# Latent heads: q and k multiplied straight into transposed form, rotary columns eight heads at a time on VectorE, other banks

## The chip, the cores and the metric

The kernel runs on one core of a Trainium2 chip. The core has a matrix engine (TensorE, PE in the profile), two engines for elementwise work (VectorE, DVE; ScalarE, ACT), GpSimd (POOL), SyncE (SP), which issues most transfers, and 16 DMA engines. Matrix products read SBUF and write to eight PSUM banks; a matrix product takes a *stationary* operand of 128 x 128 and a *moving* one of 128 rows and up to 512 columns.

The metric is the time of one execution in microseconds (us) of device time; the time before is the median of three runs. Beside these there is one profiled execution, from which the trace comes.

## The reference

One encoder layer for 256 tokens of width 4096, all in float32. A combined projection of the normalised input gives a query latent (1024 columns), a key-value latent (512), a rotary key (64), q, k, v of a dilated attention (2048 each) and two gates. The part that the change touches is the latent attention of 16 heads:

```python
q_a = jnp.einsum('bsr,re->bse', rms_norm(c_q, g_q_latent[i]), w_uq[i])
q_a = q_a.reshape(B, S, MLA_HEADS, QK_NOPE + QK_ROPE)          # 16 heads, 128 + 64 columns
q_nope, q_pe = q_a[..., :QK_NOPE], apply_rope(q_a[..., QK_NOPE:], positions)
kv = jnp.einsum('bsr,re->bse', rms_norm(c_kv, g_kv_latent[i]), w_ukv[i])
kv = kv.reshape(B, S, MLA_HEADS, QK_NOPE + V_HEAD)             # 16 heads, 128 + 128 columns
k_nope, v_a = kv[..., :QK_NOPE], kv[..., QK_NOPE:]
k_pe = jnp.broadcast_to(apply_rope(k_rope, positions)[:, :, None, :], (B, S, MLA_HEADS, QK_ROPE))
y_a = mla_attention(jnp.concatenate([q_nope, q_pe], axis=-1),
                    jnp.concatenate([k_nope, k_pe], axis=-1), v_a)   # dense softmax
y_a = rms_norm(y_a.reshape(B, S, MLA_WIDTH), g_out_mla[i]) * jax.nn.silu(gate_a)
```

After it come the output projection, a gated embedding with a 4096 x 4096 gate, and a final norm.

## The kernel before

**Precision.** Every float32 operand is split in two parts, `hi` (rounded to the format that TensorE multiplies at its fast rate) and `lo` (the rest). `split` (line 244) does it with one ACT copy and one DVE subtraction. `mm` (262) makes three products of them: hi by hi, hi by lo, lo by hi. Weights arrive by DMA in `raw` buffers (four of them), are split, and are multiplied; a step of the weight stream is one `raw` buffer, as a rule 128 x 1024 values.

**Blocks.** The large projections run as blocks of 1024 columns (`Block`, 994). Most rows of a block are *plain* steps of eight products of 512 columns (in four banks); some pairs of rows are *fast* ones, which make seven products instead of eight out of sums of the operands (four banks more) and cost DVE more work. `spread` sets their order from the number of fast pairs (`FAST_QKV`, `FAST_G`, `FAST_O`), the number of leading plain steps (`LEAD_...`) and of closing ones. When the last fast step has run, `..._mid` adds the extra banks into SBUF; at the end `..._done` does the rest. The order of the stages is: dilated q, k, v (six blocks, `d_mid`, `d_done`); the latent columns (four narrower chunks, `done_a`), beside which the dilated heads run; four gate blocks; the latent heads; two half chunks and three blocks of the output projection, two half chunks more; the last gate.

**Who sets the order.** The program is written engine by engine in a fixed order that the kernel itself plans. `Clock` (67) keeps an estimate of each engine's time, and every operation is recorded through `emit`, so that all rows of the profile have line 176. Steps of the weight stream go one after the other; between their products `tick` resumes the small tasks (evictions, attention heads, norms) whose inputs should be ready by the estimate. A task that `yield`s waits for its turn; `flags`, `locks`, `take` and `give` hold what must come first and which bank is in use. `turned` hands out one of two banks for transposes.

**Latent columns.** `done_a(i)` (504) evicts a chunk of latent columns with the norm factor of x, transposes it on PE and multiplies by the gains into `cT["q"]` and `cT["kv"]`, which are both transposed: latent index on the partitions, tokens on the columns. The last call rotates the key on POOL (`rotate`, 340), computes the norm factors `rq` and `rkv`, transposes the rotated key twice over and sets the flag "latents".

**Latent heads.** For each of eight pairs of heads there is a chunk of `w_uq` (384 columns: two heads of 128 + 64) and one of `w_ukv` (512 columns). The latents are the stationary operand, the weights move; the results stand with tokens on the partitions. `done_uq(i)` (677) scales by `rqs`, rotates the 64 rotary columns of two heads on POOL, doubles them with an ACT copy, transposes them (four transposes) and splits them; `done_uk(i)` (710) scales and splits v and scales k. Then `attend` (571) runs one head: two transposes of q and two of k, a split of 512 columns, scores (three products for q and k, two for the rotary part, for each of two row tiles), softmax, transposes of the weights, output. The query chunk's evictions wait for heads two pairs back, since the buffers of a pair are used in turn.

**Other places touched.** `load_res` (917) loads the residual by POOL's queue for the output projection; `half_o`, `done_o` (959, 969) end its half chunks; `y_sums` (1136) makes the sums for the fast pairs of the output projection.

Of the kernel before, what the change touches and what calls it, by code (L numbers as in the profile page):

```python
# [11 lines left out]
F32 = mybir.dt.float32  # L12
# [6 lines left out]
P = 128  # L19
S = 256  # L20
# [189 lines left out]
def encoder_layer(ctx: ExitStack, tc: tile.TileContext, x, p, positions, g_mix, w_in, g_q_latent, w_uq,  # L210
# [129 lines left out]
    def rotate(dst, src, tmp, h):  # L340

        half = ROPE // 2
        for t in range(NT):
            c = cc[:, t].unsqueeze(1).to_broadcast([P, h, ROPE])
            s1 = ss[:, t, :half].unsqueeze(1).to_broadcast([P, h, half])
            s2 = ss[:, t, half:].unsqueeze(1).to_broadcast([P, h, half])
            nc.gpsimd.tensor_tensor(dst[:, t], src[:, t], c, op=ALU.mult)
            nc.gpsimd.tensor_tensor(tmp[:, t, :, :half], src[:, t, :, half:], s1, op=ALU.mult)
            nc.gpsimd.tensor_tensor(tmp[:, t, :, half:], src[:, t, :, :half], s2, op=ALU.mult)
        nc.gpsimd.tensor_tensor(dst, dst, tmp, op=ALU.add)  # L350

# [152 lines left out]
    def done_a(i):  # L504
        def task(ps):
# [20 lines left out]
            if i == 2:  # L526
                kv = slot("B0", [2, 4, S], F32R)
                cT["kv"] = kv[:, 0], kv[:, 1]
            for lo, key, o, m in {0: ((0, "q", 0, 2), (2, "q", 2, 1)), 1: ((0, "q", 3, 2), (2, "q", 5, 1)),
                                  2: ((0, "q", 6, 2), (2, "kv", 0, 1)), 3: ((0, "kv", 1, 2), (2, "kv", 3, 1))}[i]:  # L530
                tag = yield from turned()
                tp = bank(tag, [2, S])
                for k in range(m):
                    for t in range(NT):
                        nc.tensor.transpose(tp[:, k, t * P:(t + 1) * P], c[:, t, (lo + k) * P:(lo + k + 1) * P], ident)
# [7 lines left out]
            kpe, rk = slot("B7a", [2, NT, 2, ROPE]), slot("B7b", [NT, 2, ROPE])  # L543
            for t in range(NT):
                for d in range(2):
                    nc.gpsimd.tensor_copy(kpe[:, 1, t, d], c[:, t, 384:448])
            rotate(rk, kpe[:, 1], kpe[:, 0], 2)
            tot = stat(2 * NT).rearrange("p (a t) -> p a t", a=2)
            nc.vector.tensor_tensor(tot[:, 0], sums[:, 0], sums[:, 1], op=ALU.add)
            nc.vector.tensor_tensor(tot[:, 0], tot[:, 0], sums[:, 2], op=ALU.add)  # L550
            nc.vector.tensor_tensor(tot[:, 1], sums[:, 3], sums[:, 4], op=ALU.add)
            yield from rsqrt_mean(rq, tot[:, 0], Q_LORA)
            nc.vector.tensor_scalar(rqs, rq, (NOPE + ROPE) ** -0.5, None, op0=ALU.mult)
            yield from rsqrt_mean(rkv, tot[:, 1], KV_LORA)
# [16 lines left out]
    def attend(h, q_src, k_src, pe, v, y, dil):  # L571
# [4 lines left out]
        tag = yield from turned()  # L576
        tp = bank(tag, [4, P])
        for t in range(NT):
            nc.tensor.transpose(tp[:, t], q_src(t), ident)
            nc.tensor.transpose(tp[:, NT + t], k_src(t), ident)  # L580
        flags.add(("took", dil, h))
        yield
        yield from take(f"T{h % 2}")
        qk = slot(f"T{h % 2}", [2, 4 * P], F32R)
        split(qk[:, 0], qk[:, 1], tp.rearrange("p a b -> p (a b)"))
        give(tag)
        if dil:
            flags.add(("read", h))
        yield
# [3 lines left out]
        for t in range(NT):  # L593
            a = tuple(qk[:, i, t * P:(t + 1) * P] for i in range(2))
            b = tuple(qk[:, i, S:] for i in range(2))
            mm(s[:, t], a, b, True, pe is None)
            if pe is not None:
                both = pe[0]()[:, t * P:(t + 1) * P]
# [3 lines left out]
        give(f"T{h % 2}")  # L602
# [72 lines left out]
    pairs = {}  # L675

    def done_uq(i):
        def task(ps):
            if i == 0:
                E["q"] = slot("Ah2", [2, NT, 2, NOPE + ROPE])  # L680
                E["kq"] = slot("Al2", [2, 1024])
                E["pe"] = slot("T5", [2, 2, S], F32R)
            while i > 1 and not all(("scored", 0, 2 * i - 3 - n) in flags for n in range(2)):
                yield
            q, kq = E["q"][:, i % 2], E["kq"][:, i % 2]
            pairs[i] = {"q": q, "kq": kq}
            for t in range(NT):
                nc.scalar.activation(q[:, t].rearrange("p h c -> p (h c)"), ps[t], AF.Copy, scale=rqs[:, t:t + 1])
            give(*ps.tags)
            both = kq[:, 512:].rearrange("p (t h d r) -> p t h d r", t=NT, h=2, d=2)  # L690
            rotate(both[:, :, :, 0], q[:, :, :, NOPE:], both[:, :, :, 1], 2)
            yield
            nc.scalar.activation(both[:, :, :, 1], both[:, :, :, 0], AF.Copy)
            yield
            tag = yield from turned()
            tp = bank(tag, [2, S])
            for h in range(2):
                for t in range(NT):
                    nc.tensor.transpose(tp[:, h, t * P:(t + 1) * P], both[:, t, h].rearrange("p d r -> p (d r)"),
                                        ident)  # L700
            yield
            pe = E["pe"][:, i % 2]
# [1121 lines left out]
```

## Time and profile before

| | us |
|---|---|
| median of three runs | 1932.27 |
| the runs | 1930.42 to 1932.83 |
| the profiled execution | 1933.49 |
| its span, first to last instruction | 1931.7 |
| mean granted clock of TensorE in it | 0.997 |

The profiled execution's time holds its span and 1.8 us around it. In the profile's rows a name stands for all tiles with it, without numbers: `m`, `s`, `o`, `t` are banks, `Ah`, `Al`, `B`, `T` are places in SBUF with several uses, `hi` and `lo` parts of weights, `raw` weights as they came, `st` small statistics. A row of a timeline has the start, the duration, the engine, the operation with output and inputs, and in brackets the idle time of the engine before it with what ended that. Matmuls are pipelined: a row's duration is longer than the distance to the next start, so the distance is what counts. A row of the waits has the engine, the tile it worked on, what it waited for, the total, how often, and the longest. A row of the stretches has, for each engine, busy us and the number of instructions, then the granted clock, the DMA engines' share and GB/s.

### The profile page before, as it was taken

The numbers are of one execution on the slowest core, as the hardware profiler recorded it, in microseconds if no ns is written. First come the engines' busy times: TensorE is split into PE (matmuls) and PEld (weight loads), VectorE is DVE, ScalarE is ACT, GpSimd is POOL, SyncE is SP. The second block draws the span as 40 slices with busy tenths as digits, with TensorE's granted clock in tenths as the row PEclk, the third lists the DMA queues.
The fourth block names the chain that finished last, engine by engine and source line by source line (L and its number), as shares of the span: only waits on it lengthen the run. The fifth ranks groups of instructions, "written<-read, shape, count | busy, mean of one in ns | idle before, by whom it ended". The sixth has DMA issues, their size and how long they took to land.

```text
span 1931.7 us, 25573 instructions
## 1 busy us (share of the span) xinstructions
PE 1902.9 (99%) x9227; PEld 1614.5 (84%) x9227; DVE 1639.1 (85%) x2270; ACT 1130.2 (59%) x1556; POOL 75.2 (4%) x123
## 2 busy tenths in 40 slices
PE   9999999999999999999999999999999999999997
PEld 7878888888899988888888888888888788888887
DVE  6999989998877789899998767898887989989865
ACT  7655556565577756556556656655555556666543
POOL 1000000000000110000001222100000000000000
PEclk9999999999999999999999999999999999999999
DMA  8666666666554566666666434766656566566665
GB/s 274 185 197 216 212 200 205 194 215 192 184 151 138 147 186 194 196 209 192 218 197 187 124 106 131 251 197 200 199 194 200 172 200 221 191 218 206 206 195 176
DMA packets 134191, 370.58 MB, mean 192 GB/s; under 512 B 11909, under 2 KB 45809, under 8 KB 133809
## 3 DMA queue, kind: packets, MB, share of 16 engines
q1 hardware_dynamic: 132176, 361.82, 59.6%
q0 software_dynamic: 1888, 7.14, 1.1%
q8 instruction: 72, 1.18, 0.3%
q14 instruction: 55, 0.44, 0.1%
HBM read 364.72 MB, written 4.19 MB: 191 GB/s over the span
## 4 chain that ended last, share of the span: by engine, by line
PE 80%; DVE 11%; issue 3%; ACT 3%; DMA 2%; POOL 1%; SPq 0%; DVEq 0%; ACTq 0%; POOLq 0%
PE m L176 44%; PE t L176 17%; PE s L176 10%; PE o L176 9%; DVE B L176 4%; DVE lo L176 3%; DVE T L176 1%; DVE Al L176 1%; ACT hi L176 1%; POOL Al L176 1%; DMA raw<-in_w_ple_gate_dram 1%; DMA raw<-in_w_in_dram 1%; DVE Ah L176 1%; ACT T L176 1%; DVE st L176 1%
## 5 line engine op out<-in xcount | busy, mean ns | idle before, releaser
L176 ACT ACTIVATE hi<-raw 128x1024 fp32r<-128x1024 f32 (+3 forms) x486 | 467.4, 969 | 347.0 <-PE m L176 107.8
L176 DVE TENSOR_TENSOR lo<-raw,hi 128x1024 fp32r<-128x1024 f32 (+3 forms) x486 | 537.9, 1115 | 137.2 <-ACT hi L176 133.8
L176 PE MATMUL m<-hi,Ah 128*128 128x512 f32 (+3 forms) x815 | 298.2, 380 | 0.9 <-ACT hi L176 0.9
L176 PE MATMUL m<-hi,Al 128*128 128x512 f32 (+3 forms) x807 | 289.7, 371 | 0.0
L176 PE MATMUL m<-lo,Ah 128*128 128x512 f32 (+2 forms) x702 | 261.8, 373 | 0.3 <-DVE lo L176 0.2
L176 PE MATMUL m<-hi,B 128*128 128x512 f32 (+2 forms) x772 | 244.7, 371 | 0.8 <-ACT Ah L176 0.4
L176 DVE TENSOR_TENSOR B<-raw,B 128x1024 fp32r<-128x1024 f32 (+2 forms) x209 | 189.0, 913 | 15.1 <-ACT B L176 13.2
L176 PEld LDWEIGHTS m<-hi,Ah 128*128 128x128 f32 x815 | 153.3, 188 | 22.9 <-ACT hi L176 1.6
L176 PEld LDWEIGHTS m<-hi,Al 128*128 128x128 f32 x807 | 151.4, 188 | 21.3 <-ACT hi L176 0.3
L176 ACT ACTIVATE B<-raw 128x1024 fp32r<-128x1024 f32 (+1 forms) x125 | 115.8, 934 | 80.5 <-DMA raw<-in_w_in_dram 22.4
L176 PEld LDWEIGHTS m<-hi,B 128*128 128x128 f32 x772 | 143.3, 188 | 21.1 <-ACT Ah L176 0.8
L176 PEld LDWEIGHTS m<-lo,Ah 128*128 128x128 f32 x702 | 132.2, 188 | 20.2 <-DVE lo L176 3.1
L176 PE MATMUL m<-lo,B 128*128 128x512 f32 (+2 forms) x386 | 142.2, 368 | 1.2 <-DVE lo L176 1.2
L176 PE MATMUL m<-B,Ah 128*128 128x512 f32 (+1 forms) x327 | 94.4, 382 | 0.0
L176 ACT ACTIVATE hi<-B 128x1024 fp32r<-128x1024 f32 x65 | 68.2, 1058 | 38.5 <-PE m L176 15.7
L176 DVE TENSOR_TENSOR lo<-B,hi 128x1024 fp32r<-128x1024 f32 x65 | 78.2, 1220 | 10.3 <-ACT hi L176 9.4
L176 DVE TENSOR_TENSOR T<-t,T 128x512 fp32r<-128x512 f32 (+2 forms) x73 | 49.8, 685 | 41.3 <-ACT T L176 40.9
L176 PE MATMUL t<-hi,Ah 128*128 128x512 f32 (+1 forms) x226 | 84.4, 388 | 0.0
L176 PEld LDWEIGHTS m<-lo,B 128*128 128x128 f32 x386 | 72.8, 189 | 11.5 <-DVE lo L176 2.3
L176 DVE TENSOR_TENSOR T<-raw,T 128x512 f32<-128x512 f32 (+2 forms) x101 | 77.6, 777 | 3.9 <-ACT T L176 2.5
L176 PE MATMUL t<-hi,Al 128*128 128x512 f32 x194 | 74.3, 392 | 0.0
L176 PE MATMUL t<-lo,Ah 128*128 128x512 f32 (+1 forms) x185 | 72.1, 390 | 0.0
(456 smaller groups left out, 3879.1 us busy)
## 6 DMA issues: line engine op xcount, KB each, us to landing
raw<-in_w_in_dram SPq DMA_DIRECT2D x320, 512.0 KB, 4.3
raw<-in_w_out_dram SPq DMA_DIRECT2D x128, 512.0 KB, 4.5
raw<-in_w_ple_gate_dram SPq DMA_DIRECT2D x128, 512.0 KB, 4.6
raw<-in_w_in_dram SPq DMA_DIRECT2D x48, 384.0 KB, 3.3
raw<-in_w_uq_dram SPq DMA_DIRECT2D x32, 384.0 KB, 3.3
raw<-in_w_ukv_dram SPq DMA_DIRECT2D x16, 512.0 KB, 3.9
raw<-in_w_in_dram SPq DMA_DIRECT2D x16, 448.0 KB, 3.5
T<-in_x_dram POOLq DMA_DIRECT2D x8, 512.0 KB, 9.8
```

The lines of the kernel that those rows point to most:

```text
L176: return do(out, *rest, **named)
```

## The change

For each pair of heads `query_unit` and `key_unit` take the place of the two chunks. In them the weights of one head are the stationary operand and the transposed latents move (256 columns, one per token), so that q and k come out transposed and the transposes and the split in `attend` fall away for the latent heads; v comes out as before. The loads of `w_uq` take the 128 columns of each head by themselves (rows of 512 bytes, two DMAs a step). A step here is a pair of steps that share a product: the first only loads and splits, the second multiplies both. `turn_steps` multiplies the rotary columns of eight heads at once, in four steps after pairs 0 and 4 (rows of 256 bytes, two DMAs a step); its `done` rotates them on DVE from the banks, doubles and transposes them for four heads at a time; for the second eight heads it waits until the heads whose place it takes have been scored. `rotate` on POOL is gone; the key is rotated on DVE. Instead of scaling q, its norm factor goes into the softmax (a product on DVE for the maximum, a scale in the exponential); that of kv is applied to the latent before its transposes, which therefore come later in `done_a`.

Besides: the banks of the gates, the heads and the output projection are dealt out in another order; the first block of q has three closing plain steps for two; the first gate block has four fast pairs for five and 14 leading steps for 12; the residual of two chunks is loaded earlier; `done_o` releases its banks before the squares; `y_sums` starts after the second rotary run and uses other places.

```diff
@@ done_a
+                T7["held"] = slot("B7a", [4, HD])
+                for t in range(NT):
+                    nc.scalar.activation(T7["held"][:, t], c[:, t, 256:384], AF.Copy)
+            if i == 3:
+                nc.vector.tensor_tensor(own, c[:, :, 384:], cc, op=ALU.mult)
...
+                yield from rsqrt_mean(rkv, tot[:, 1], KV_LORA)
+                for t in range(NT):
+                    nc.scalar.activation(c[:, t, :384], c[:, t, :384], AF.Copy, scale=rkv[:, t:t + 1])
+                    nc.vector.tensor_scalar(held[:, t], held[:, t], rkv[:, t:t + 1], None, op0=ALU.mult)
...
-            rotate(rk, kpe[:, 1], kpe[:, 0], 2)
@@ attend
+            nc.vector.tensor_tensor(nmax, nmax, rqs, op=ALU.mult)
             for t in range(NT):
-                nc.scalar.activation(e[:, t], s[:, t], AF.Exp, bias=nmax[:, t:t + 1], accum_out=l[:, t:t + 1])
+                nc.scalar.activation(e[:, t], s[:, t], AF.Exp, bias=nmax[:, t:t + 1], scale=rqs[:, t:t + 1],
+                                     accum_out=l[:, t:t + 1])
@@ query_unit
+        def load(r, j):
+            for h in range(2):
+                nc.sync.dma_start(r.rearrange("p a (b c) -> p (a b) c", c=2 * NOPE)[:, :, h * NOPE:(h + 1) * NOPE],
+                                  src[4 * P * j:4 * P * (j + 1), 2 * i + h, :NOPE].rearrange("(k p) c -> p k c", p=P))
+
+        def product(held, ps):
+            for h in range(2):
+                for kt in range(8):
...
+                    mm(ps[0][:, h], w, [q[:, kt] for q in cT["q"]], kt == 0, kt == 7)
+                    tick()
@@ key_unit
+        def product(held, ps):
+            for h in range(2):
+                for kt in range(4):
...
+                    mm(ps[0][:, h], w, [q[:, kt] for q in cT["kv"]], kt == 0, kt == 3)
+                    tick()
             for t in range(NT):
...
+                    mm(ps[1][:, t].rearrange("p (h c) -> p h c", h=2), [q[:, kt, t * P:(t + 1) * P] for q in cT["kv"]], w,
+                       kt == 0, kt == 3)
@@ turn_steps
+                for k in range(2):
+                    kt = 2 * j + k
+                    nc.sync.dma_start(box[0][:, k].rearrange("p (h r) -> p h r", h=8),
+                                      src[kt * P:(kt + 1) * P, 8 * n:8 * (n + 1), NOPE:])
...
+                nc.vector.tensor_tensor(own, ps[t], turn[2], op=ALU.mult)
+                nc.vector.tensor_tensor(other[..., :half], ps[t][..., half:], turn[0], op=ALU.mult)
+                nc.vector.tensor_tensor(other[..., half:], ps[t][..., :half], turn[1], op=ALU.mult)
+                give(tags[t])
+                twice = slot("T1", [8, 2, ROPE])
+                nc.vector.tensor_tensor(twice, *(a.unsqueeze(2).to_broadcast([P, 8, 2, ROPE]) for a in (own, other)), op=ALU.add)
+                yield
+                for j in range(2):
+                    while n and not all(("scored", 0, 4 * j + m) in flags for m in range(4)):
+                        yield
@@ load_res
-        while not all(("head", 0, h) in flags for h in range(HEADS)):
+        before = {6: ("pe", 1), 7: ("scored", 0, HEADS - 1)}.get(c)
+        while not (before in flags if before else all(("head", 0, h) in flags for h in range(HEADS))):
@@ y_sums
-        while not {("yT", 3), ("uq", 7)} <= flags:
+        while not {("yT", 3), ("pe", 1)} <= flags:
@@ the order of the stages
-    FAST_G, LEAD_G = (5, 7, 7, 7), (12, 6, 6, 4)
+    FAST_G, LEAD_G = (4, 7, 7, 7), (14, 6, 6, 4)
...
-        order = spread(FAST_QKV[n], LEAD_QKV[n], (2, 2, 2, 2, 2, 5)[n])
+        order = spread(FAST_QKV[n], LEAD_QKV[n], (3, 2, 2, 2, 2, 5)[n])
...
     for i in range(8):
-        for ch in (Chunk(cols(w_uq, 384 * i, 384), 8, 384, lhs_c("q"), ("m0", "m1"), done_uq(i), lambda j: ["latents"]),
-                   Chunk(cols(w_ukv, 512 * i, 512), 4, 512, lhs_c("kv"), ("m2", "m3"), done_uk(i),
...
+        steps.extend(query_unit(i, *next_banks(1)))
+        if i in (0, 4):
+            steps.extend(turn_steps(i // 4, next_banks(2)))
+        steps.extend(key_unit(i, next_banks(2)))
```

More of the change, by code (lines that the diff above doesn't have):

```diff
@@ L534, in task @@
                     for t in range(NT):
[L535 removed]
+                        nc.tensor.transpose(tp[:, k, t * P:(t + 1) * P], block(t, lo + k), ident)
                 yield
@@ L692, in task @@
[L692 to L702, printed above, removed]
-            nc.scalar.activation(pe, tp, AF.Copy)
@@ L960, in task @@
         def task(ps):
-            while c not in x1:
-                yield
+            yield from awaited(("res", c))
             for t in range(NT):
```

262 lines of the change are left out of this document (166 added, 96 removed).

## The prediction

> **What bounds the kernel now.** I read the engine totals first, then the stretches, then what TensorE (PE) waited for, then single places in order of time.
>
> ```profile
> PE 1902.9 (99%) x9227; PEld 1614.5 (84%) x9227; DVE 1639.1 (85%) x2270; ACT 1130.2 (59%) x1556; POOL 75.2 (4%) x123
> ```
>
> PE is the bound almost everywhere; VectorE (DVE) is the only engine close behind. The stretches show where PE is not full, and where DVE is:
>
> ```profile
> core 0: us, PE busy (x) PEld busy (x) DVE busy (x) ACT busy (x) POOL busy (x), PEclk, DMA share, GB/s
> 100.00:200.00 100.00, 97.48 (x423) 80.25 (x422) 97.71 (x129) 55.89 (x65) 0.00 (x0) 0.98 0.65 209
> ...
> 300.00:400.00 100.00, 100.00 (x442) 82.82 (x442) 93.28 (x108) 58.38 (x61) 0.00 (x0) 1.00 0.66 206
> ...
> 900.00:1000.00 100.00, 100.00 (x442) 82.58 (x441) 93.63 (x110) 60.81 (x64) 0.00 (x0) 1.00 0.65 202
> ...
> 1100.00:1200.00 100.00, 96.98 (x579) 87.06 (x579) 66.83 (x108) 60.65 (x130) 25.79 (x44) 1.00 0.41 123
> ...
> 1033.80:1209.00 175.20, 169.25 (x1000) 152.27 (x998) 126.26 (x200) 109.59 (x229) 41.98 (x69) 1.00 0.44 133
> ```
>
> PE loses time after 100 and from 1033.8 to 1209, the latent heads: 5.95 us idle there, with GpSimd (POOL) at work. In that stage DVE has 48.9 us free, ACT 65.6. In the dilated blocks and the gates (100:200, 300:400, 900:1000) DVE has only 2 to 7 us free in 100. The waits of PE over the whole span, largest first:
>
> ```profile
> PE t L176 <- ACT Al L176: 3.7, 5, 1.0
> PE o L176 <- DVE B L176: 2.5, 1, 2.5
> PE m L176 <- DVE lo L176: 2.2, 3, 1.2
> PE t L176 <- DVE T L176: 1.9, 3, 1.3
> ...
> PE m L176 <- DVE Al L176: 0.7, 1, 0.7
> PE s L176 <- DVE T L176: 0.6, 2, 0.4
> ...
> PE s L176 <- ACT T L176: 0.3, 1, 0.3
> ```
>
> So a change can win little by waits: these are 12 us, beside 2 at the start. What it does to the PE's own work decides as much.
>
> **PE's own work.** The pitch (start to start) of each kind of matmul, from places where nothing waits:
>
> ```profile
> 1120.46 0.51 PE L176 MATMUL m<-hi,B 128*128 128x384 f32 x2
> ...
> 1121.50 0.33 PE L176 MATMUL m<-hi,B 128*128 128x384 f32 x1
> ...
> 1123.55 0.60 PE L176 MATMUL t<-ident,T 128*128 128x128 f32 x4
> 1123.90 0.42 PE L176 MATMUL m<-hi,B 128*128 128x384 f32 x1
> ...
> 1886.19 0.28 PE L176 MATMUL m<-hi,Al 128*128 128x256 f32 x1
> ...
> 1888.35 0.28 PE L176 MATMUL m<-hi,Al 128*128 128x256 f32 x1
> ```
>
> Six matmuls of 384 columns start between the first two rows: 1.04/6 = 0.173 us. Four transposes take 0.35 us. Eighteen matmuls of 256 columns lie between the last two: 2.16/18 = 0.120. The stretch 300:400 has 512 columns alone: 100/442 = 0.226.
>
> Counted in the order of instructions before and after: 192 matmuls of 512 columns (keys and values) go; 96 of 512 (rotary columns, two runs of 48) come; the first gate block has one fast pair fewer, which is one product more, 3 of 512: net 93 fewer, -21.0 us. 384 of 384 columns go: -66.4. 768 of 256 come: +92.2. The two transposes of q and two of k per head go: 16 groups of four, -5.6. The rotary transposes stay at eight groups. Sum **-0.8 us**: the same columns are multiplied, in narrower pieces which cost 0.01 to 0.02 us more for each cut, and the transposes about pay for that. So "straight into transposed form" wins nothing in PE work, and the rest hangs on waits.
>
> **The rotary wait.** Before, each pair of heads sends its rotary columns over POOL; one pair, all engines:
>
> ```profile
> 1149.01 0.46 POOL L176 TENSOR_TENSOR Al<-Ah,cc 128x128 f32<-128x128 f32 x1 [13.54 <-ACT Ah L176]
> ...
> 1152.45 0.39 PE L176 MATMUL m<-hi,B 128*128 128x512 f32 x1
> 1152.63 0.72 POOL L176 TENSOR_TENSOR Al<-Al 128x256 f32<-128x256 f32 x1
> ...
> 1153.38 0.42 ACT L176 ACTIVATE Al<-Al 128x256 f32<-128x256 f32 x1 [1.80 <-POOL Al L176]
> ...
> 1153.86 0.66 PE L176 MATMUL t<-ident,Al 128*128 128x128 f32 x4 [1.01 <-ACT Al L176]
> ```
>
> POOL takes 4.3 us (1149.01 to 1153.35) for seven small operations; then ACT copies, then PE transposes, 1.2 us after it could have (1152.45 to 1153.86, less 0.23). The view counts 3.7 us in five such waits; counted from the last start, as here, instead of the last modelled end, I put 4.5 us on them. The change removes POOL and this copy: **-4.5**. The removed split of q and k (waits on T by s) gives **-0.9** (0.6 + 0.3).
>
> What takes its place on DVE, by the groups of the stretch 1033 to 1210:
>
> ```profile
> L176 DVE TENSOR_TENSOR T<-t,T 128x512 fp32r<-128x512 f32 x30 | 20.6, 688 | 21.4 <-ACT T L176 21.2
> ...
> L176 DVE TENSOR_SCALAR Al<-m,st 128x256 f32<-128x256 f32 x16 | 7.1, 478 | 2.2 <-PE m L176 1.1 <-ACT B L176 0.9
> L176 DVE SCALAR_TENSOR_TENSOR B<-m,st,B 128x256 fp32r<-128x256 f32 x16 | 6.9, 474 | 0.0
> ```
>
> Four rotations come (two runs, two row tiles), each one 512-wide, two 256-wide and one 1024-wide operation (at most twice a 512-wide): 0.7 + 0.9 + 1.4 = 3.0 us, 12 in all; also 24 splits of 512 (three a pair, 16.5) and 16 products of two columns, under 0.5 each. The 16 splits of q and k (11) and the last two groups (14) go. Net under +12 us of DVE in a stage with 48.9 free; ACT loses the copies and gets no more splits than DVE. Cover: the other weight matmuls. If it is gone, one 3.0 us rotation stands before a head. There are such places: the second run may write its transposed rotary queries only when heads 0 to 7 are scored, and head 8 waits for all of it. I take **+1**, between 0 and two rotations with their transposes (6).
>
> **The loads.** 16 loads of 512 KB with rows of 256 bytes (8 steps of two) and 32 with rows of 512 take the place of rows of 1536. The trace has no row for such packets. From 300:400, packets of 4096 bytes move 206/(0.66 x 16) = 19.5 GB/s per engine. If the rate held, a rotary step of 512 KB would cost 1.7 us; PE spends 12 x 0.226 = 2.7 on it. From above: if a short packet took as long as one of 1536 bytes at that rate (0.079 us), 2048 of them on 16 engines would take 10.1 us. Four raw buffers ahead hide one late load, not four in a row. Gains are excluded; I take **+0.5** near the lower end, as 1536 and 4096 bytes show the same rate (1100:1200: 123/(0.41 x 16) = 18.8). The Trainium skill, "DMA: Bandwidth & Descriptors", speaks against the change: by its Specifications line rate is lost under 512 bytes, and by "Why small descriptors are slow" a 256-byte packet carries 27% overhead; by that, an estimate, a step takes 2.1 us and the sum stays; no row here shows it.
>
> **The first block's end.** It gets three closing plain steps for two.
>
> ```profile
> 100.72 1.22 DVE L176 TENSOR_TENSOR lo<-raw,hi 128x1024 fp32r<-128x1024 f32 x1
> 101.86 2.19 DVE L176 SCALAR_TENSOR_TENSOR B<-t,st,B 128x512 f32<-128x512 f32 x3
> 103.96 1.40 DVE L176 SCALAR_TENSOR_TENSOR B<-o,st,B 128x512 f32<-128x512 f32 x2
> 105.28 1.21 DVE L176 TENSOR_TENSOR B<-raw,B 128x1024 fp32r<-128x1024 f32 x1
> ...
> 102.51 0.39 PE L176 MATMUL s<-hi,Al 128*128 128x512 f32 x1
> 105.42 0.50 PE L176 MATMUL o<-hi,Ah 128*128 128x512 f32 x1 [2.52 <-DVE B L176]
> ...
> 106.45 0.63 PE L176 MATMUL t<-lo,Ah 128*128 128x512 f32 x1
> ...
> 109.44 0.58 PE L176 MATMUL s<-hi,Al 128*128 128x512 f32 x1
> ```
>
> PE waits 2.7 us for the eviction of bank o; then seven matmuls take 2.99 us, 0.43 each, at half the clock: 1.4 more, with their neighbours 1.8 (clock 0.98 in 100:200). In the new order one weight split (1.14 us from its start at 100.72 to the next row) stands behind the eviction instead of ahead. DVE is busy throughout, so the eviction comes 1.1 us earlier, no more; a gap of 1.6 us is left. The 1.3 us gap at 696 (next fence) brings no slow matmuls behind it, so I let the 1.8 go too. But DVE stays full to 200, and PE, 2.9 earlier, finds weights less ahead: I take **-2.0**, between 0 and -4.5. The Trainium skill, "TensorE: Matmul & The Clock Gate", Part 1, puts the drop of the clock behind an idle window of 3.4 us that runs freely; a gap of 2.7 that halves the rate disagrees. By that rule a gap of any such length could still straddle a window; then the term is -0.2.
>
> **Latent columns to gates.**
>
> ```profile
> 695.83 0.37 PE L176 MATMUL m<-hi,Al 128*128 128x448 f32 x1
> 696.32 0.33 PE L176 MATMUL t<-ident,T 128*128 128x128 f32 x1
> 697.94 0.55 PE L176 MATMUL t<-ident,T 128*128 128x128 f32 x3 [1.29 <-DVE T L176]
> ```
>
> Before, PE goes straight to transposes of what ACT and DVE are still copying out: 0.3 us (0.49 where even 512 columns take 0.226) and 1.5 (1.62 less a transpose). In the new order these stand some 13 us of matmuls later, behind the normalisation of kv, so **-1.7**. Late next is "latents", which the gate needs only after 14 plain steps (38 us).
>
> **The rest.** The sums over y start after the rotary run instead of the last query: the 0.7 us wait on DVE Al goes (**-0.7**); it would fall back if DVE met them with rotations. Fewer fast pairs in the first gate relieve DVE by 3 us that PE doesn't wait for: 0. The other banks, the squares after the release in the last half chunks, and the earlier residual loads on POOL's queue (idle by then) I take at 0, within 1.1 either way (half of the 2.2 us that PE waits for lo). SP's queue:
>
> ```profile
> L176 SPq DMA_DIRECT2D raw<-in_w_uq_dram x32: 367/368/378, 1021.4 to 1167.9; - x32
> ```
>
> It gets 48 for these 32, 0.37 us each: six more in 175, behind loads that nothing waits for yet.
>
> **The sum.** -0.8 - 4.5 - 0.9 + 1 + 0.5 - 2.0 - 1.7 - 0.7 = **-9.1 us** on a profiled execution of 1933.5 (span 1931.7 and 1.8 around it), 1924.4; it lies 1.2 above the median of the runs, so about 1923. The stage is longer than its matmuls by pitch: 384 x 0.173 + 192 x 0.226 + some 234 x 0.120 (scores and outputs) + 39 x 0.35 + some 40 x 0.226 of the next step = 161 of 175 us, where the waits shown explain some 5.5. Part of these short restarts stands at transposes and evictions that go; I add -1: **1922**.
>
> **Rivals.**
> - *Deeper gain.* If POOL's latency set the whole order of the stage, the 8 us that I leave of its 14 go as well: 1914. For: DVE and ACT have room. Against: most of these are restarts of 0.1 us that weights' splits cause in any order.
> - *Handed back.* PE arrives sooner at blocks where DVE is 93 to 98% busy and waits for lo instead. Only the stage's 5.4 us and the 0.8 stay, less the 1.5 of new costs: 1928; with 2 us lost in the gates too, 1930.
> - *Slower: packets.* Loads with rows of 256 bytes take a time per packet. At 10.1 us for a step against 2.7, four in a row cost 7.4 x 4 less the lead of four buffers (10.8), 19 us, twice: 1960. It decides from 5.4 us a step on (0.042 us a packet); above 6.7 us (0.052) it has eaten the gain. For: nothing like it is in the trace. Against: the even rate of 1536 and 4096.
> - *Doesn't do what it says.* The narrower matmuls miss their pitch because every one loads new weights: at PEld's mean of 1614.5/9227 = 0.175 us instead of 0.120, 768 x 0.055 = 42 us, 1964. Against: the 256-column rows at 1886 also load each time.
>
> **How the numbers follow.** The forecast has 0.55 with its own range 1915 to 1928, deeper 0.20, handed back 0.13, packets 0.09, narrow pitch 0.03. Under 0.2% (3.9 us) a measurement can't tell a change from none. Faster: 0.55 + 0.20 + a third of 0.13, less a little: 0.79; same 0.09; slower 0.12. The range goes from 1909 (deeper, with the first block's full 4.5) to 1932, leaving out the last two rivals.
>
> **What would show it.** Right: no POOL operation but the sums of squares between 1030 and 1200; no wait of t on ACT Al; the latent stage 6 to 8 us shorter; no gap where latent columns end; the gap at 102 near 1.6 us without 0.43 us matmuls behind. Wrong: ACT hi waiting for DMA raw from in_w_uq by more than a microsecond in the rotary steps; 256-column matmuls over 0.13 us apart; m waiting on DVE lo between 110 and 200 or in the gates; s of the ninth head waiting on DVE or ACT T.

## The result, and the profile after

| | before | after |
|---|---|---|
| median of six runs each, same chip | 1932.55 us | 1923.25 us |
| the runs | 1930.42 to 1933.41 | 1922.69 to 1927.51 |
| the profiled execution, its span | 1933.49, 1931.7 | 1922.69, 1920.9 |

The ratio is 0.9958, 95% interval 0.9945 to 0.9970: faster by 0.42%, 5.8 to 10.6 us. Forecast was 1922.0.

Engine totals, then stretches of the changed kernel (busy us and instructions of each engine, granted clock, share of the DMA engines, GB/s), then all that TensorE (PE) waited for by tile:

```profile
PE 1897.0 (99%) x9454; PEld 1615.9 (84%) x9454; DVE 1635.0 (85%) x2270; ACT 1115.9 (58%) x1518; POOL 40.8 (2%) x56
```

```profile
100.00:200.00 100.00, 99.96 (x440) 82.11 (x439) 97.80 (x129) 55.64 (x65) 0.00 (x0) 1.00 0.67 212
300.00:400.00 100.00, 100.00 (x442) 82.78 (x442) 93.15 (x108) 58.49 (x61) 0.00 (x0) 1.00 0.65 204
1100.00:1200.00 100.00, 98.16 (x711) 91.44 (x710) 75.31 (x132) 56.02 (x111) 10.36 (x10) 1.00 0.43 129
```

```profile
PE m L176 <- DVE B L176: 3.5, 4, 1.4
...
PE m L176 <- ACT hi L176: 1.4, 2, 0.9
PE m L176 <- DVE lo L176: 1.1, 5, 0.3
PE m L176 <- ACT Al L176: 0.9, 1, 0.9
PE m L176 <- DVE Al L176: 0.8, 1, 0.8
...
PE t L176 <- DVE T L176: 0.5, 2, 0.3
```

The reader is to see three things. PE has 227 instructions more and is busy 5.9 us less. In 100:200 it goes from 97.48 to 99.96 at full clock, in 1100:1200 from 96.98 to 98.16, while 300:400, which the change does not touch, stays. The waits on POOL's chain (t on ACT Al, 3.7 us) and on the eviction of bank o (2.5) are gone, and others stand in the list: m on DVE B (3.5 for 0.8 before) and on ACT Al, which was not there.

Since the change moves work past the edges of any fixed stretch, I also cut each trace at points that every kernel has: the first matmul of the latent columns (384 columns), the last of them (448), the first of the latent heads, the last 512-column matmul of the two half chunks behind the heads, and the end. "Lost" is the distance from each matmul's start to the next beyond the pitch of its kind (0.227, 0.174, 0.120 us for 512, 384, 256 columns), summed. The loss of the first 50 us stands apart: it is 4.9 to 7.6 us in one execution or another of either kernel, so it says nothing of an edit. All runs told of below are in the table; names with b_ are the kernel before with an edit, with a_ the changed kernel with one.

```
us             lost in    rest, to first   latent    gates   heads and     rest to
               first 50   latent column    columns           half chunks   the end
before            5.1         512.1         178.6    338.0      218.5       679.4
b_trail3          6.8         508.5         178.8    337.9      218.4       679.6
b_rot_dve         7.3         512.0         178.6    340.0      216.1       679.4
b_small           4.9         508.9         178.8    338.0      216.2       678.4
after             5.0         508.6         178.9    336.8      212.0       679.7
after_again       5.1         508.8         178.8    336.8      212.0       684.3
a_trail2          7.2         512.0         178.7    336.7      211.9       679.9
a_gate5           5.1         509.1         178.8    341.4      211.9       684.5
a_banks           7.2         508.5         178.9    339.0      211.9       684.2
a_rot_pool        7.2         508.6         178.8    337.1      222.2       678.7
a_rows256         7.6         508.8         178.5    337.4      211.9       685.5
a_ysums           5.6         508.8         178.8    337.0      211.5       683.5
a_res_squares     5.1         509.0         178.9    337.2      211.5       682.2
a_run_early       5.2         508.4         178.8    337.4      211.6       677.8
```

Before to after: -3.5 up to the latent columns, -1.2 in the gates, -6.5 in the heads, and in the rest +0.3 in one execution and +4.9 in the other. The first four are the same in both executions of the changed kernel to 0.3 us; the last is where these two executions differ, by 4.6 us.

### The profile page after: what moved, and what is told of

Its sections match the earlier page's. It is cut to its first block, busy times and chain, and to the rows that moved or that the text cites. A ratio compares the mean times of both kernels' runs of the same rounds, so it can differ in the third digit from the quotient of the medians.

```text
span 1920.9 us, 25936 instructions
## 1 busy us (share of the span) xinstructions
PE 1897.0 (99%) x9454; PEld 1615.9 (84%) x9454; DVE 1635.0 (85%) x2270; ACT 1115.9 (58%) x1518; POOL 40.8 (2%) x56
## 2 busy tenths in 40 slices
DMA packets 159024, 370.61 MB, mean 193 GB/s; under 512 B 28548, under 2 KB 70640, under 8 KB 158640
## 4 chain that ended last, share of the span: by engine, by line
PE 90%; DVE 5%; DMA 2%; ACT 1%; issue 1%; SPq 0%; DVEq 0%; ACTq 0%
PE m L176 51%; PE t L176 17%; PE s L176 11%; PE o L176 11%; DVE lo L176 1%; DVE T L176 1%; DMA raw<-in_w_out_dram 1%; DVE B L176 1%; DVE Al L176 1%; ACT hi L176 1%; ACT T L176 0%; DVE st L176 0%; DMA raw<-in_w_in_dram 0%; DMA raw<-in_w_ple_gate_dram 0%; DVE Ah L176 0%
## 5 line engine op out<-in xcount | busy, mean ns | idle before, releaser
L176 ACT ACTIVATE hi<-raw 128x1024 fp32r<-128x1024 f32 (+3 forms) x453 | 438.1, 976 | 344.5 <-PE t L176 90.0
L176 DVE TENSOR_TENSOR lo<-raw,hi 128x1024 fp32r<-128x1024 f32 (+3 forms) x453 | 502.3, 1118 | 112.5 <-ACT hi L176 109.4
L176 PE MATMUL m<-hi,Ah 128*128 128x512 f32 (+2 forms) x840 | 310.0, 381 | 3.5 <-DVE B L176 2.1
L176 PE MATMUL m<-lo,Ah 128*128 128x512 f32 (+3 forms) x722 | 269.3, 373 | 0.8 <-DVE lo L176 0.8
L176 PE MATMUL m<-hi,B 128*128 128x512 f32 (+1 forms) x654 | 206.1, 365 | 1.0 <-DVE B L176 1.0
L176 PEld LDWEIGHTS m<-hi,B 128*128 128x128 f32 x654 | 120.0, 189 | 19.6 <-issue 1.4
L176 PE MATMUL m<-lo,B 128*128 128x512 f32 (+1 forms) x327 | 118.9, 364 | 0.2 <-DVE lo L176 0.2
L176 PEld LDWEIGHTS m<-B,Ah 128*128 128x128 f32 x389 | 66.6, 189 | 11.1 <-DVE B7b L176 0.2
L176 PE MATMUL m<-B,Al 128*128 128x512 f32 (+1 forms) x286 | 75.8, 345 | 0.0
L176 PEld LDWEIGHTS m<-lo,B 128*128 128x128 f32 x327 | 61.8, 189 | 10.2 <-DVE lo L176 1.6
L176 ACT ACTIVATE hi<-B 128x1024 fp32r<-128x1024 f32 x51 | 53.7, 1057 | 22.3 <-issue 8.6
```

The costliest lines, as they stand in the source:

```text
L176: return do(out, *rest, **named)
```

## The experiments

The runs were made on several chips, so a time is to be read beside the kernel before on the same chip, which is what each ratio is taken from.

**The third closing step of the first block, alone and taken away.** In the list of closing steps:

```diff
-        order = spread(FAST_QKV[n], LEAD_QKV[n], (2, 2, 2, 2, 2, 5)[n])
+        order = spread(FAST_QKV[n], LEAD_QKV[n], (3, 2, 2, 2, 2, 5)[n])
```

b_trail3 (the edit in the kernel before):

> The kernel before with three closing plain steps in the first block and nothing else. Third step alone: no gap after 102 us, no matmuls 0.43 us apart, 4 us less than before, 1928.5. Prediction's size: 1930.5 with a gap of about 1.6 us left. Something else of the change: 1932.5.

a_trail2 (the edit taken back in the changed kernel):

> The changed kernel with the first block's closing plain steps back at two. If the third closing step alone took away the wait at 102 us and the half-rate matmuls behind it: the gap of 2 to 3 us and about eight matmuls 0.43 us apart are back, lost time of PE in 100 to 150 us goes from 0.4 to about 4.4 us, and the run is 4 us longer, 1927. If the step is worth the 2.0 us of the prediction: 1925, with a gap but no slow matmuls, or a gap of about 1.1 us more. If other parts of the change moved the eviction: 1923, no gap.

b_trail3: 1931.87 us beside 1934.26 before, ratio 0.9984 (0.9974 to 0.9994). a_trail2: 1929.06, ratio 0.9970 (0.9958 to 0.9981). The medians alone don't part 2.0 us from 4.0; the traces do. Lost time in 100 to 150 us: 4.36 before, 0.38 in b_trail3, 0.38 after, 4.37 in a_trail2. The third step alone does it; at 89 to 91 us it gives 0.5 back, so the stretch is 3.5 us shorter. Timeline of a_trail2, where the gap is back with eight matmuls 0.43 us apart behind it, and of the changed kernel, where PE runs on:

```profile
104.39 0.39 PE L176 MATMUL s<-hi,Al 128*128 128x512 f32 x1
107.29 0.50 PE L176 MATMUL o<-hi,Ah 128*128 128x512 f32 x1 [2.51 <-DVE B L176]
...
108.58 0.61 PE L176 MATMUL t<-hi,Al 128*128 128x512 f32 x1
108.99 0.63 PE L176 MATMUL t<-hi,Ah 128*128 128x512 f32 x1
```

```profile
101.45 1.40 DVE L176 SCALAR_TENSOR_TENSOR B<-o,st,B 128x512 f32<-128x512 f32 x2
...
102.75 0.39 PE L176 MATMUL s<-hi,Al 128*128 128x512 f32 x1
102.98 0.43 PE L176 MATMUL o<-hi,Ah 128*128 128x512 f32 x1
```

The eviction of bank o starts at 101.45 for 103.96: 2.5 us earlier, not 1.1. The missing part is far from the gap. Before, DVE stood idle at 65 us, once, and no longer after:

```profile
66.46 1.23 DVE L176 TENSOR_TENSOR lo<-raw,hi 128x1024 fp32r<-128x1024 f32 x1 [1.25 <-ACT hi L176]
```

1.1 (one split behind the eviction) and 1.25 (this idle time) make 2.4 of the 2.5.

**The rotations on the other engine, both ways.** b_rot_dve puts the small rotations of the kernel before on VectorE; a_rot_pool puts the two large ones of the changed kernel on GpSimd behind an ACT copy:

```diff
@@ b_rot_dve, rotate
-            nc.gpsimd.tensor_tensor(dst[:, t], src[:, t], c, op=ALU.mult)
+            nc.vector.tensor_tensor(dst[:, t], src[:, t], c, op=ALU.mult)
...
@@ a_rot_pool, turn_steps, done
-                nc.vector.tensor_tensor(own, ps[t], turn[2], op=ALU.mult)
+                nc.scalar.activation(got, ps[t], AF.Copy)
+                give(tags[t])
+                nc.gpsimd.tensor_tensor(own, got, turn[2], op=ALU.mult)
...
```

> The kernel before with the same small rotations (two heads at a time, seven operations) on VectorE instead of GpSimd. If GpSimd's 4.3 us for them are what TensorE waits for: the waits of t on ACT Al (3.7 us in five) all but go, the latent stage is 3.5 to 4.5 us shorter, 1928 to 1929. If VectorE's queue takes the place of GpSimd's time, or the heads are late for another reason, the waits stay: 1931 to 1933. If GpSimd sets the order of the whole stage (the deeper gain): 1920 to 1924.

> The changed kernel with its two rotations of eight heads on GpSimd, after an ACT copy out of the banks (by 0.88 us for 256 columns, some 7 us a row tile where VectorE takes 3). If doing eight heads at once is what hides them: no wait of t longer than 0.3 us, stage within 1 us, 1923 to 1924.5. If the engine matters wherever it stands in the chain: waits of s or t for the rotary columns of heads 0 and 8 come to 5 to 10 us, 1928 to 1933.

b_rot_dve: 1934.54 beside 1934.26, ratio 1.0001 (0.9992 to 1.0011). a_rot_pool: 1931.65, ratio 0.9989 (0.9980 to 0.9998). Waits of PE in 1010 to 1210, first of b_rot_dve, then of a_rot_pool:

```profile
PE s L176 <- ACT T L176: 1.5, 2, 1.2
PE t L176 <- DVE T L176: 1.3, 1, 1.3
...
PE t L176 <- ACT Al L176: 0.2, 1, 0.2
```

```profile
PE m L176 <- DVE B L176: 6.7, 1, 6.7
PE t L176 <- POOL T L176: 4.0, 2, 3.5
```

In b_rot_dve the waits on ACT Al fall from 3.7 us to 0.2, as the theory had it, but only 2.4 us of the stage go. The first rows of its list are softmax steps: at 1084.64 the rotation of a pair stands on DVE ahead of a weight split and of the scaling of the exponentials, whose transposes wait 1.27 us for it, and the scores of the next head come late in turn. So a small rotation on VectorE trades one wait for another. The loss of 2.0 us in the gates is another matter (below). In a_rot_pool the heads take 10.2 us longer: slow rotations are not hidden by doing eight heads at once. What the change has is both: few rotations, and the fast engine.

**The small version.** b_small is the kernel before with three closing steps and the heads' rotations on VectorE, that of the key left on GpSimd:

```diff
-    def rotate(dst, src, tmp, h):
+    def rotate(dst, src, tmp, h, on=None):
+        on = on or nc.vector
...
-            rotate(rk, kpe[:, 1], kpe[:, 0], 2)
+            rotate(rk, kpe[:, 1], kpe[:, 0], 2, nc.gpsimd)
```

> The kernel before with two small edits: three closing plain steps in the first block, and the rotations of two heads at a time on VectorE, that of the key left on GpSimd. If the loss of 1.8 us at 733 us in the run with all rotations on VectorE came from the key's rotation ahead of the sums for the gate's fast steps: it is gone here, the latent stage (1000 to 1200 us) loses about 12 us as there, for 14, and with 3.7 us of the first block the kernel is 5 to 6 us faster than before, ratio 0.9970 to 0.9975. If the loss at 733 came from elsewhere: 3.5 to 4 us, ratio 0.998. The whole change is at 0.9955 to 0.9958; what is left to it is the transposed form, the run of eight heads and the order of banks.

1928.21 beside 1932.47, ratio 0.9979 (0.9970 to 0.9988): less than the expected 5 to 6 us. The loss in the gates is gone (338.0), so it was the key's rotation. The small edits give 3.2 us up to the latent columns and 2.3 in the heads; the whole change gives 6.5 in the heads. How the other 4.2 divide between the transposed form, doing eight heads at once and the smaller edits beside them, no run shows: the first two were not tried apart. The order of banks has no part in them (a_banks below has 211.9 in the heads, as the changed kernel).

**Short rows.** a_rows256 cuts each load of 128 query columns in two of 64:

```diff
-            for h in range(2):
+            for b in range(4):
+                h, lo = b // 2, b % 2 * half
...
-                                  src[4 * P * j:4 * P * (j + 1), 2 * i + h, :NOPE].rearrange("(k p) c -> p k c", p=P))
+                                  src[4 * P * j:4 * P * (j + 1), 2 * i + h, lo:lo + half].rearrange("(k p) c -> p k c", p=P))
```

> The changed kernel with every load of 128 query columns cut in two of 64: rows of 256 bytes for 512, twice the transfers. If the even rate holds down to 256 bytes: landing stays near 4 us, no wait of ACT on raw_q over 1 us, time within 1 us of the changed kernel, 1923 to 1924. If such rows cost a time per packet of 0.042 us or more (the rival of the prediction): a query step of 512 KB takes over 5.4 us, waits on raw_q of several us each, over 1935.

1926.93, ratio 0.9968 (0.9955 to 0.9980): longer than the 1923 to 1924 expected, but not in this stage (heads 211.9 us for 212.0); its traced execution loses more in the first 50 us and in the rest. The transfers of the changed kernel, then of a_rows256 (count, size, median from issue to landing):

```profile
raw_q<-in_w_uq_dram SPq DMA_DIRECT2D x32, 256.0 KB, 4.0
...
raw_r<-in_w_uq_dram SPq DMA_DIRECT2D x16, 256.0 KB, 3.7
```

```profile
raw_q<-in_w_uq_dram SPq DMA_DIRECT2D x64, 128.0 KB, 3.1
```

Rows of 256 bytes (raw_r) land in 3.7 us, as fast as rows of 512 (raw_q), and 33,000 more packets under 512 bytes (61,829 for 28,548) cost the stage nothing. ACT waits for raw_q once, 2.0 us, where it waits 1.1 us in the changed kernel; at neither does PE wait longer than its short restarts. The rival of the packets falls.

PE's longest wait where these loads arrive, 0.84 us at 1058 in the changed kernel, is no load either. The weights of that product had been split by 1056; the second key product needs the bank that the first rotation has read until 1059.00:

```profile
1058.25 0.75 DVE L176 TENSOR_TENSOR T<-m,ss 128x256 f32<-128x256 f32 x2
...
1059.14 0.47 PE L176 MATMUL m<-B,hi 128*128 128x256 f32 x2 [0.68 <-ACT Ah L176]
```

The row of PE names ACT, whose copy of another bank ends 0.1 us later, at 1059.10. With all query loads cut in two the wait is the same, 0.83.

The Trainium skill, "DMA: Bandwidth & Descriptors", Specifications, sees line rate lost under 512 bytes; in this stage, where the DMA engines are 43% busy, no run shows a cost in time.

**Two edits that the prediction priced at nothing.** a_gate5 gives the first gate block its five fast pairs and 12 leading steps back; a_banks gives gates, heads, output projection and last gate the banks of before:

```diff
@@ a_gate5
-    FAST_G, LEAD_G = (4, 7, 7, 7), (14, 6, 6, 4)
+    FAST_G, LEAD_G = (5, 7, 7, 7), (12, 6, 6, 4)
@@ a_banks
-    G_BANKS = "m2", "m3", "s", "o", "m0", "m1", "t0", "t1"
+    G_BANKS = X_BANKS
...
```

> The changed kernel with the first gate block at five fast pairs and 12 leading steps, as before. One product fewer by the fast pair (3 matmuls of 512, -0.7 us) and 3 us more DVE work. Prediction (DVE work that nobody waits for, 0): 1922.5. If the fourteen leading steps are what covers the later normalisation of the latent key columns: a wait at 735 to 760 us of 1 to 3 us, 1924 to 1926.

> The changed kernel with the order of the banks of the kernel before in the gates, the heads, the output projection and the last gate. Prediction (banks 0 within 1.1): 1922 to 1924.5, lost time moves between 1180, 1537, 1624, 1636 and 1801 us with a sum near zero. If the order of banks carries part of the gain: 2 us or more longer, 1925 to 1928, with the 1.0 us at 1537 and the 1.4 at 1801 back. If it costs (the 1.55 at 1180, the 2.0 at 1624 and 1635 come from it): 1920 to 1921.

a_gate5: 1931.96, ratio 0.9991 (0.9982 to 1.0001): nearly the whole gain is gone, 4.6 us of it in the gates (341.4 for 336.8); the rest of its trace (684.5) is as long as in after_again, where nothing was edited. a_banks: 1929.25, ratio 0.9979 (0.9970 to 0.9988). Timelines where the gates begin, a_gate5 first, then a_banks:

```profile
727.52 0.39 PE L176 MATMUL o<-hi,Al 128*128 128x512 f32 x1
728.88 0.49 PE L176 MATMUL m<-B,Ah 128*128 128x512 f32 x1 [0.98 <-ACT B L176]
731.02 0.79 PE L176 MATMUL m<-B,Ah 128*128 128x512 f32 x1 [1.64 <-DVE B L176]
731.61 0.63 PE L176 MATMUL m<-B,Al 128*128 128x512 f32 x1
```

```profile
694.56 0.37 PE L176 MATMUL m<-hi,Al 128*128 128x448 f32 x1
695.01 0.56 ACT L176 ACTIVATE m<-m,st 128x384 f32<-128x384 f32 x1
...
695.73 0.73 PE L176 MATMUL m<-B,Ah 128*128 128x512 f32 x2 [0.81 <-ACT m L176]
```

In a_gate5 the leading plain steps end before the first fast weights are made: these may be split only when the sums for the fast steps are done, and the sums stand on DVE behind the rotation of the key and the normalisation of kv that the change puts there. PE loses 3.05 us in the two gaps and then runs six matmuls at 0.43. DVE, in the same stretch, on the last sum and on the first fast weights behind it:

```profile
728.35 0.69 DVE L176 TENSOR_TENSOR T<-B,T 128x512 fp32r<-128x512 f32 x1 [0.70 <-ACT T L176]
...
730.28 0.69 DVE L176 TENSOR_TENSOR B<-raw,B 128x512 fp32r<-128x512 f32 x1
```

Two more plain steps (5.5 us) and one fast pair fewer cover that; which of the two does it was not tried. In b_rot_dve, with 12 steps, the key's rotation alone costs 2.0. In a_banks the first gate matmuls need the banks that ACT is still emptying of latent columns: two gaps, of 0.98 and 0.62 us beyond the pitch, bring back 1.6 of the 1.8 us that the moved transposes saved (650 to 700 us lost 2.91 us; 2.90 before, 1.10 after). A wait of 3.5 us opens at 1247 as well, behind the half chunks.

**The sums over y, the residual loads, the squares.** a_ysums starts the sums after the last query pair; a_res_squares loads all residuals after the last head and releases the banks of `done_o` after the squares, as before:

```diff
@@ a_ysums
-        while not {("yT", 3), ("pe", 1)} <= flags:
+        while not {("yT", 3), ("uq", 7)} <= flags:
@@ a_res_squares
-        before = {6: ("pe", 1), 7: ("scored", 0, HEADS - 1)}.get(c)
+        before = None
...
```

> The changed kernel with the sums over y started after the last query pair, as before. By the prediction's step they would fall back on a wait of m on DVE Al, +0.7: 1924. If the early sums are what stands on DVE ahead of the eviction at 1180 (1.55 us): that wait goes, 1921.5 to 1922.5. If the two waits at 1265 and 1267 (2.1 us) come from the sums they stay or go with it; if from other loads they stay.

> The changed kernel with the residual of the two half chunks loaded after the last head and the squares ahead of the release of the banks, as before. Prediction (0 within 1.1): 0 to 1.1 us either way. If the release is what takes away the 1.0 us at 1537: it is back, +1. If the late squares are what stands ahead of the evictions at 1624 and 1635 (2.0 us): these go, -2. If the early loads matter: a wait at the end of the latent heads, 1200 to 1250 us, of 1 to 3 us.

a_ysums: 1927.41, ratio 0.9968 (0.9958 to 0.9979): the wait at 1180 goes, as the second theory said, but the stage is only 0.5 us shorter (211.5), since shorter waits open in it, and the two waits of 1265 (2.1 us after) are 3.4 at 1276 instead. So the time is not the 1921.5 to 1922.5 of that theory. a_res_squares: 1925.56, ratio 0.9958 (0.9946 to 0.9970): no change to be seen in time; the 1.0 us at 1537 is back (at 1527 here), the waits at 1625 and 1637 stay.

**The changed kernel again, and the second rotary run earlier.** a_run_early:

```diff
     for i in range(8):
+        if i == 4:
+            steps.extend(turn_steps(1, next_banks(2)))
         steps.extend(query_unit(i, *next_banks(1)))
-        if i in (0, 4):
-            steps.extend(turn_steps(i // 4, next_banks(2)))
+        if i == 0:
+            steps.extend(turn_steps(0, next_banks(2)))
```

> The changed kernel once more, beside the others on one chip, as the measure for them. If the lost 1.4 us at 1801 us (a wait for a transfer of the last gate, there in the kernel before and in most variants) is left out of the first trace by chance, it is here; the places at 1058, 1180, 1265, 1624 and 1635 us come again with the same sizes. Ratio to the kernel before 0.995 to 0.997.

> The changed kernel with the second rotary run ahead of the fifth query pair instead of behind it, 5.8 us of products earlier. If heads 8 to 15 are late by that run and the 1.55 us at 1180 us is its end (evictions of the seventh pair wait for head 9): the ninth head scores 3 to 6 us earlier, the wait at 1180 is under 0.4, 1.5 to 2.5 us less than the changed kernel. If the wait at 1180 is the sums over y ahead of the eviction on DVE: it stays, no change within 0.5 us.

after_again: 1924.84, ratio 0.9955 (0.9942 to 0.9967). a_run_early: 1920.87 (1919.89 to 1921.23), ratio 0.9932 (0.9920 to 0.9945), 4.0 us below the changed kernel beside it (1922.53 to 1927.54), the best of all. But not by my reason: the ninth head scores 0.7 us earlier, not 3 to 6. What it moves is the sums over y. The wait at 1180 in the changed kernel:

```profile
1175.79 0.69 DVE L176 TENSOR_TENSOR T<-Ah 128x512 f32<-128x512 f32 x1
1176.51 1.57 DVE L176 TENSOR_TENSOR T<-T 128x128 f32<-128x128 f32 x4
1178.00 1.21 DVE L176 TENSOR_TENSOR lo<-raw,hi 128x1024 fp32r<-128x1024 f32 x1
1179.13 1.21 DVE L176 TENSOR_TENSOR Al<-raw,Al 128x1024 fp32r<-128x1024 f32 x1
1180.27 0.68 DVE L176 TENSOR_TENSOR Ah<-m,Ah 128x512 fp32r<-128x512 f32 x1
1180.87 0.68 DVE L176 TENSOR_TENSOR B<-m,B 128x512 fp32r<-128x512 f32 x1
...
1181.60 0.50 PE L176 MATMUL m<-hi,Ah 128*128 128x512 f32 x1 [1.39 <-DVE B L176]
```

The eviction of v (B from m) stands behind a sum over y (T from Ah, four of 128) and two weight splits; the half chunk needs the bank. And the residual loads on GpSimd's queue, before, after, after_again and a_run_early:

```profile
1219.34 5.81 POOL L176 DMA_DIRECT2D T<-in_x_dram  x8
```

```profile
1218.66 1.45 POOL L176 DMA_DIRECT2D T<-in_x_dram  x2
1255.46 3.61 POOL L176 DMA_DIRECT2D T<-in_x_dram  x5 [35.35 <-DVE B L176]
```

```profile
1255.84 3.60 POOL L176 DMA_DIRECT2D T<-in_x_dram  x5 [35.45 <-DVE B L176]
```

```profile
1214.95 5.05 POOL L176 DMA_DIRECT2D T<-in_x_dram  x7
```

The change gives the sums over y the place T1, which the fourth of the eight residual loads also takes. The last sum leaves it at 1255 (the split B from T), so this load and the four behind it on the queue start then together: 2.6 MB beside the weights. The stretch 1255:1275, in the same order of kernels:

```profile
1255.00:1275.00 20.00, 20.00 (x90) 16.57 (x89) 17.63 (x29) 11.18 (x13) 0.00 (x0) 1.00 0.60 188
```

```profile
1255.00:1275.00 20.00, 18.29 (x80) 14.58 (x79) 15.83 (x19) 8.96 (x10) 3.61 (x5) 1.00 0.91 318
```

```profile
1255.00:1275.00 20.00, 17.93 (x72) 14.12 (x71) 15.57 (x18) 9.22 (x11) 3.60 (x5) 0.91 0.88 318
```

```profile
1255.00:1275.00 20.00, 20.00 (x90) 16.57 (x89) 17.86 (x20) 10.81 (x14) 0.00 (x0) 1.00 0.68 224
```

At 318 GB/s the DMA engines are 90% busy, and the weights of a fast step come late:

```profile
1265.90 1.06 ACT L176 ACTIVATE Al<-raw 128x1024 fp32r<-128x1024 f32 x1 [7.18 <-DMA raw<-in_w_out_dram]
...
1267.01 0.49 PE L176 MATMUL m<-Al,Ah 128*128 128x512 f32 x1 [0.95 <-ACT Al L176]
1268.27 1.43 PE L176 MATMUL m<-Al,Ah 128*128 128x512 f32 x5 [0.76 <-DVE Al L176]
```

In a_run_early the last sum ends at 1211.7, the loads go at 1215, and PE loses nothing here. Over all runs: where the five loads go in 1254 to 1267 (after twice, a_trail2, a_gate5, a_banks, a_rows256, a_ysums, a_res_squares) the rest takes 679.7 to 685.5 us; where the loads go by 1235 (the four before, a_rot_pool, a_run_early) 677.8 to 679.6. Seven of those eight late executions have the two waits, 1.8 to 3.4 us together between 1265 and 1281. The eighth, a_banks, has loads at 1254 and no wait behind them; there PE had already stood 3.5 us at 1247, before the loads. The burst itself accounts for 2.2 us (after) and 4.2 (after_again) at 1265 to 1273. The other 2.6 between the two executions lie at 1396 (0.6), 1797 (1.1) and smaller places; whether these are late weights of the same cause or chance is open: a wait of 1.4 us near 1797 is in the kernel before too. Another place for the sums than T1, which would test it alone, was not tried.

## Why the prediction was right, point by point

The forecast of 1922.0 is 1.25 from 1923.25, and its place among the cases (the likeliest one) was right. Not all its terms were.

- *PE's own work, -0.8.* The counts are right (93 of 512 and 384 of 384 columns fewer, 768 of 256 more); with the pitches 0.227, 0.174 and 0.120 they give -1.4, the difference being rounding. Where one 256-column product of the latent stage follows another, the median of 732 distances is 0.120 us and 19 are over 0.13, so the rival of the missed pitch falls. "Straight into transposed form" wins next to nothing in PE work, as said.
- *The rotary wait, -4.5, split waits -0.9, bubble +1, loads +0.5, restarts -1: together -4.9.* Lost time between 1000 and 1200 us goes from 14.04 to 9.68: -4.4. The stage with the half chunks is 6.5 us shorter (6 to 8 predicted). No wait of t on ACT Al is left, and POOL does sums of squares alone. In the 9.68 stand 1.55 at 1180, which belong to the sums over y; without them it would be -5.9 by subtraction, but a_ysums, which has no wait there, still loses 9.06. The +1 of the rotations is 1.2: 0.34 where transposes wait behind the second rotation (1136), and the 0.84 at 1058. The loads, taken at +0.5, cost PE nothing that can be seen; ACT's one wait of 1.1 us for raw_q, just over the microsecond named as a sign of being wrong, does not reach PE. (The estimate of 2.1 us for a step adds 27% to 1.7; an overhead that is 27% of the whole makes 2.3, still under the 2.7 of products.) That the engine alone makes the rotary term, as the sum reads, is not so: b_rot_dve gets 2.4 by it.
- *The first block's end, -2.0.* The mechanism was right, the size wrong: -4.0 at the place, 3.5 in the stretch. The step that failed is "DVE is busy throughout, so the eviction comes 1.1 us earlier, no more". DVE had 1.25 us idle at 65 us, 37 us ahead of the gap, outside the rows that the prediction shows. With the gap its half-rate matmuls went too. No gap is left where 1.6 us were predicted, so whether one of 1.6 us would have brought slow matmuls stays open.
- *Latent columns to gates, -1.7.* Lost there: 2.90 to 1.10, -1.8. But the sentence that the transposes' place gives it is only half the cause: without the new banks 1.6 comes back, without the further plain steps and with the fifth fast pair 4.6 are lost.
- *The rest, 0 within 1.1.* As a net change from the kernel before this held for squares and residual loads. As prices of the edits it failed for two: the fast pair and leading steps ("0") are worth 4.6 us in the gates, the 0.7 that their additional product costs already taken off, and the banks 1.6 there and 3.5 at 1247. They win nothing over before; they keep the other terms. The prediction named what covers "latents" (14 plain steps), not what else DVE owes by then.
- *Sums over y, -0.7.* Wrong in sign. The wait on DVE Al is 0.8 after for 0.7 before, the sums stand ahead of an eviction, and by way of T1 they hold up the residual loads. The prediction had "earlier residual loads on POOL's queue (idle by then) at 0": the queue was idle, but the place that a load writes was not free, and the loads behind it waited in order.

So the sum came so close in part by luck, by errors that cancel: 1.5 us too little gain for the first block and 0.6 for PE's work, against the sums over y, forecast at -0.7, which cost 1.55 us of waiting at 1180 and 2.2 or 4.2 behind the loads. By the traces, what lies behind the heads is 0.3 us longer in one execution and 4.9 in the other; the six runs spread from 1922.69 to 1927.51, and the median lies near their lower end. Part of the "handed back" rival is true in this: DVE meets the heads' end with more to do. The deeper gain did not come: 9.7 us are still lost between 1000 and 1200, of which 4.9 are restarts of 0.2 and less.

## What to carry to other kernels

Price an edit that seems neutral (an order of banks, one more plain step, a lead) by what it protects: take it away from the changed kernel in mind, and see which new work would then be late. A buffer given to a new use holds back every load that wants it and, on a queue in order, every load behind that one; look for when its last reader ends, then for what the burst collides with. To say how much earlier an operation can come, look for its engine's idle time back to the last point where it waited, not only near the gap.

## What was not expected of the hardware

The half rate of TensorE comes after less idle time than I thought, and not each time. One gap of 2.7 us at 102 brought eight matmuls 0.43 us apart in all three executions that have it (before, a_trail2, b_rot_dve). Two gaps of 1.48 and 1.03 us brought eight in after_again (1269.48 to 1272.46), and 1.19 and 1.03 in a_gate5; 1.28 and 1.03 in a_rows256 and even 2.34 and 1.03 in a_ysums brought none. In the heads, 1.43 and 1.35 brought eight (256 columns, 0.213 apart) in b_small and the same two gaps none in b_rot_dve. The Trainium skill, "TensorE: Matmul & The Clock Gate", Part 1, describes a window that runs freely, and the chance in these rows agrees; so does its 3.4 us for the way back (8 x 0.427). That the idle time must fill such a window does not: 2.2 us of idle time, in two parts with a matmul between, were enough.
